# Gate and up of a gated feed-forward: weights as the stationary operand, 256 tokens moving

## The chip, the cores and the metric

One core of a Trainium2 chip runs the whole program. The metric is device time in microseconds (us), from runs of the compiled program; a profile of one execution stands beside them. In the profile PE is TensorE's matmul, PEld its weight load, DVE VectorE, ACT ScalarE, POOL GpSimd and SP SyncE, whose queue issues the loads.

## The reference, cut to what matters

The model is two blocks of two layers each on x of 256 tokens by 1024 features. A layer of the first block is a feed-forward, an attention mixer and another feed-forward; a layer of the second is a mixer and a feed-forward with modulated norms. So there are six feed-forwards, each with 2816 hidden columns:

```python
def swiglu(h, w_gate, w_up, w_down):
    return (jax.nn.silu(h @ w_gate) * (h @ w_up)) @ w_down
...
        x = x + 0.5 * swiglu(h, ffn1_w_gate[l], ffn1_w_up[l], ffn1_w_down[l])
```

All of it is float32.

## The kernel before

**Products.** A float32 product is made of three float32r products: each operand is split into a high part and the rest (`xh`, `xl` for the tokens, `whi`, `wlo` for weights, `hth`, `htl` for the hidden values), and `mm3` issues high by high, high by low, low by high. Each product is one matmul instruction with its own weight load. The operand named `lhsT` is stationary (128x128), `rhs` moves.

**Tokens.** The 256 tokens are two tiles of 128. `xh` and `xl` hold the normed input transposed, 128 features by 8 k-tiles by 256 tokens. `proj` (line 609) takes 128 tokens as the stationary operand and 512 weight columns as the moving one.

**A feed-forward** (`ffn`, line 619) goes over 11 chunks of 256 hidden columns. A chunk's gate and up columns, 256 each, lie side by side in the 512 moving columns, and its weights come in two units (k-tiles 0 to 3 and 4 to 7) of 128x2048. For each token tile 24 matmuls fill one PSUM bank (tag `mm`, two of them); `post` (line 624) takes silu of the gate half on ScalarE and multiplies by the up half on VectorE into `hch`, with tokens on the partitions. `turn` (line 636) then transposes the chunk with four 128x128 transposes on TensorE into a PSUM tile (tag `tp`) and splits it from there into `hth` and `htl`, hidden columns on the partitions, which is the form that `down` (line 649) needs as its stationary operand. `down` issues 24 matmuls of 512 moving columns for a chunk, four chunks late (`LAG`), into four PSUM banks (tag `y`). Chunks 0 and 1 have an order of their own at the start, chunks 2 to 10 run in one loop (line 683); the last four `down`s come after it. The very first feed-forward has its norm's factors `r` applied after the products.

**Weights** are a stream of 1 MB units in order of use (`WStream`, up to 4 units split and 3 raw ones): SP loads a unit, ScalarE copies it into `whi`, VectorE subtracts into `wlo`, each in two halves.

**Order of the work.** `Plan` records every instruction and then issues them in the order of a list schedule with an assumed cost for each (`cost`): every engine takes, of what is ready, the most urgent. `priorities` (line 306) computes the urgencies, and keeps work beside the main products from falling more than `LATE` behind them; it knows main products by a moving width of 512 (line 317). Between products `slot` issues steps of other work that the second block needs early (tables, modulation rows).

Since a helper issues everything, all profile rows carry line L304; the tile names tell the groups apart.

Of the kernel before, what the change touches and what calls it, by code (L numbers as in the profile page):

```python
# [18 lines left out]
P = 128  # L19
# [12 lines left out]
# order of the output projections' (token tile, group of 256 columns); pools of attention's PSUM beside them  # L32
# [3 lines left out]
# engines of the copies out of PSUM, in turn  # L36
COPY = "a"
# the first two units come in CUTS pieces, FIRST of them before the second token tile; up to NCUT in two;
# splits of the others in SPLITS pieces
CUTS, FIRST, NCUT, SPLITS = 4, 2, 5, 2  # L40
# products that warm the array's clock while the first loads are under way
WARM = 8
# the list schedule
# [4 lines left out]
class Pool:  # L48
    """A tile pool whose tiles the plan knows: which slots they share and how many there are."""
# [23 lines left out]
class Plan:  # L73
    """Records the program in its order, then issues it in the order of a list schedule:
    every engine takes, of the instructions whose operands are there, the one needed soonest."""
# [72 lines left out]
    def cost(self, eng, method, args, kw, aps):  # L148
        """ns on the engine, ns on the DMA rings, activation table."""
        if method == "dma_start":  # L150
            return (1000 if eng == "gpsimd" else 475), 4 * int(np.prod(list(args[0].shape))) / 360, None
        n = max(int(np.prod(list(a.shape)[1:])) for k, a in aps)
        psum = any(a.space == PSUM for _, a in aps)
        if eng == "tensor":
            if method == "transpose":
                return 109, 0, None
            n = kw["rhs"].shape[-1]
            if kw["rhs"] is self.cold:
                return 4 * max(107, n / 1.2 + 2), 0, None
            if kw["rhs"].dtype == F32R:  # L160
                return n / 2.4 + 2.5, 0, None
            return 2 * max(107, n / 1.2 + 2), 0, None
        if eng == "scalar":
            extra = 93 * sum(1 for k, _ in aps if k in ("bias", "scale", "accum_out"))
            f = args[2] if len(args) > 2 else kw.get("func")
            return 0.833 * n + (52 if psum else 94) + extra, 0, "silu" if f == AF.Silu else "exp" if f in (AF.Exp, AF.Ln) else None
        if eng == "vector":
            fast = method in ("tensor_copy", "tensor_scalar", "memset") and not psum
            scalars = sum(1 for k, _ in aps if k not in (0, 1, "out", "in_")) if method == "tensor_scalar" else 0
            scalars += sum(1 for k, _ in aps if k == 2) if method == "scalar_tensor_tensor" else 0  # L170
            return n * (0.52 if fast else 1.042) + 68 + 62 * scalars, 0, None
        if eng == "gpsimd":
            if kw.get("op") == ALU.pow:
                return 300 + 165 * n, 0, None
            return 148 + (3.15 if method == "tensor_copy" else 2.11) * n, 0, None
        return 60, 0, None

# [1 line left out]
    def order(self, prio):  # L179
        """List schedule: every engine starts, of what can start within DELTA of the soonest, the most urgent.  # L180
        A tile may take a slot before its turn if the program's order could still go on from there."""
# [41 lines left out]
        def slot_time(i):  # L223
            """When the slots of the tiles that op i touches first are free; None: not now."""
# [81 lines left out]
    def priorities(self):  # L306
        """How long before the end an op has to start, by a schedule from the end; no later than LATE behind
        the large products it was recorded with, and the first loads in their order."""
# [3 lines left out]
        for _ in range(ITERS):  # L312
# [3 lines left out]
            for i, o in enumerate(ops):  # L316
                if o[1] == "matmul" and o[3]["rhs"].shape[-1] == 512:
                    main = p[i]
                p[i] = max(p[i], main - LATE)
# [4 lines left out]
    def backward(self, start):  # L324
        """List schedule from the end; a tile waits for the one that had its slot in the program's order."""
# [52 lines left out]
class WStream:  # L378
    """Weights in the order of their use: load ahead, split into hi + lo float32r parts ahead."""
# [9 lines left out]
    def cuts(self, i, n):  # L389
        """The first units come in pieces: the products start the sooner."""  # L390
# [12 lines left out]
    def _load(self, pieces=None):  # L403
        """The next unit, or only the next pieces of it."""
# [47 lines left out]
class Net:  # L452
# [80 lines left out]
    def rstd2(self, ss):  # L533
        """(ss[0] + ss[1] + eps) ** -0.5: the two halves' parts of a mean of squares."""
# [6 lines left out]
    def norm(self, t, gain, shift=None):  # L541
        """rms_norm(x_t) * gain (+ shift)"""
# [18 lines left out]
    def first_xT(self, t, gain):  # L561
        """xh/xl columns of token tile t := transpose of x_t * gain; the tokens' factors come after the products."""
# [28 lines left out]
    def m(self, n, name, dt=F32):  # L591
        """One of the shared 2 KB slots."""
# [16 lines left out]
    def proj(self, ps, n, t, half, u, kts=4):  # L609
        """ps[128, n] += x^T k-tiles of one weight unit [128, kts, n]."""  # L610
# [8 lines left out]
    def ffn(self, ydone, mid, pre, r=None):  # L619
# [26 lines left out]
        def mmps():  # L646
            return self.ps.tile([P, 512], F32, tag="mm", name="mm")

# [34 lines left out]
        for c in range(2, NCH):  # L683
            u = [W.next() for _ in range(2)]
            for t in range(2):
                ps = mmps()
                for half in range(2):
                    self.proj(ps, 512, t, half, u[half])
                    if t == 1:
                        W.done(u[half])  # L690
                    self.slot()
                post(c, t, ps)
                if t == 0:
                    if c == 2:
                        turn(0)
                    turn(c - 1)
# [10 lines left out]
        for t in range(2):  # L707
            for i, d in enumerate(range(NCH - LAG, NCH)):
                down(d, t, us[i])
                if t == 0 and i == 0:  # L710
# [25 lines left out]
    def slot(self):  # L736
        """Between the products of a feed-forward: one step of the work that block 2 needs early."""
# [12 lines left out]
    def copy(self, out, in_):  # L750
        """PSUM -> SBUF, on the engines in turn."""
# [27 lines left out]
    def skew(self, name, src, offset, nh, rows, n):  # L779
        """Every head's n values once per row, each row SKEW after the one before: read at SKEW - 1 they slide."""  # L780
# [5 lines left out]
    def diff_lambda(self, l):  # L786
        """-lambda on every partition; the output gain times (1 - lambda_init)."""
# [17 lines left out]
    def na_bias(self, l):  # L805
        """8 * (relative bias, or -1e30 outside the window), [token of a tile, tile, head, key]."""
# [19 lines left out]
    def prep(self, t, ps, segs, w, rope, dstT, flag):  # L826
        """Heads' norms, gains and rotations of a [128, n] projection, then its transpose."""
# [54 lines left out]
    def job(self, kind, l, h, q, k, vh, col, bias=None):  # L882
        """softmax(q k / 8 + bias) v for one head, both token tiles of queries."""
# [32 lines left out]
    def turn_p(self, p):  # L916
        """[query, (tile, key)] -> [key of a tile, (query tile, key tile, query)]"""
# [54 lines left out]
    def turn_o(self, g, flag):  # L972
        """o columns of one group of 256, transposed and split for the output projection."""
# [135 lines left out]
    def modulation(self):  # L1109
        """Rows of block 2's norms: gain * (1 + scale), shift, gate * post gain, twice per layer."""  # L1110
# [52 lines left out]
    def t5_bias(self):  # L1163
        """8 * (table[bucket(q - k)], or -1e30 above the diagonal), keys of the tile before | own tile."""
# [34 lines left out]
    def gated_residual(self, t, y, i):  # L1199
        """x_t += gate * rms_norm(y) * gain"""  # L1200
# [11 lines left out]
    def rot2(self, X, nh, t):  # L1212
        """Rotary positions on [128, nh, 32]."""
# [7 lines left out]
    def latents(self, l, t, ps, st):  # L1221
        """Norms of the latents and their transposes, rotated shared key, forget logits."""
# [27 lines left out]
    def forget(self, l, st):  # L1250
        """F, the cumulative log forget gates: min(z, 0) - log(1 + e), e = exp(-|z|), log(1 + e) = 2 artanh(e / (2 + e)); the fox biases 8 * (F[q] - F[k]), or -1e30 above the diagonal."""
# [26 lines left out]
    def qk_fox(self, t, ps, dst, st):  # L1278
        """Queries [q, 8 F, 1] and keys [k, 1, -8 F], transposed: their products are 8 (q k / 8 + F[q] - F[k])."""
# [32 lines left out]
    def latent_heads(self, t, ps, part, st):  # L1312
        """Four heads of the up-projections: queries (part 0) or keys and values (part 1), transposed."""
# [22 lines left out]
    def causal_job(self, kind, q, k, vh, col, bias, scale):  # L1336
        """Causal softmax(q k * scale + bias) v for one head; bias comes divided by the scale."""
# [30 lines left out]
    def group_norm(self, l, g0, ng):  # L1368
        """rms_norm over groups g0 .. of 256 columns of o, then transposed, times the gain, and split."""
# [188 lines left out]
def pack(inputs):  # L1558
    """Weights laid out as the units are read: every partition's part of a unit is contiguous."""
# [7 lines left out]
    def gu(g, u):  # L1567
        g = g.reshape(2, 4, P, NCH, 256).transpose(3, 0, 2, 1, 4)
        u = u.reshape(2, 4, P, NCH, 256).transpose(3, 0, 2, 1, 4)
        return np.concatenate([g, u], axis=-1).reshape(2 * NCH, P, UW)  # L1570

    stack = lambda f: np.stack([f(l) for l in range(L)])
    for i in (1, 2):
        o[f"gu{i}"] = stack(lambda l: gu(a[f"ffn{i}_w_gate"][l], a[f"ffn{i}_w_up"][l]))
# [37 lines left out]
def shape_consts():  # L1612
    """Positions, masks and multiplicities: functions of the shapes alone."""
# [51 lines left out]
```

## Time and profile before

| | |
|---|---|
| median of 3 runs | 1675.52 us (1671.84 to 1676.18) |
| profiled execution, its span | 1670.4 us; the page gives no other time for it |
| PE busy | 1646.5 us (99%), 7912 matmuls |
| PEld busy | 1346.0 us (81%), 7912 loads |
| DVE busy | 1086.1 us (65%) |
| ACT busy | 841.8 us (50%) |
| DMA | 335.78 MB, mean 201 GB/s |

The span runs from the first to the last instruction of the profiled execution. Matmuls overlap in the records (a matmul's recorded duration is longer than the distance to the next one's start), so what a matmul costs is read from the distance between starts, not from its duration.

### The profile page before, as it was taken

Reading aid. Unit: us, or ns where it says so; the run is one execution under the profiler, and the core shown is the slowest. Engines: PE = TensorE matmul, PEld = TensorE weight load, DVE = VectorE, ACT = ScalarE, POOL = GpSimd, SP = SyncE. Lnnn points to the kernel's source line nnn. Section 1 sums busy time; section 2 is a strip of 40 time slices with the busy share of each in tenths; the row PEclk is TensorE's granted clock in tenths of the full one; section 3 lists DMA queues with packets and bytes.
Section 4 is the critical chain, followed back from the end, with each engine's and each line's share of the span. In section 5 each row is a group of like instructions: output and inputs, shape, how many; then the busy total and the mean of one; then the engine's idle time right before and its main releaser. Section 6 shows DMA issues by size and latency. Waiting matters only on the chain.

```text
span 1670.4 us, 21333 instructions
## 1 busy us (share of the span) xinstructions
PE 1646.5 (99%) x7912; PEld 1346.0 (81%) x7912; DVE 1086.1 (65%) x1956; ACT 841.8 (50%) x1384; POOL 166.3 (10%) x205
## 2 busy tenths in 40 slices
PE   9989999999999999999999999999999999999998
PEld 7868877888888888887788888888888888888886
DVE  6557788577677776777857655656754476585553
ACT  6544456554444444446554444576643358664442
POOL 0000056000000000026500000120000012000000
PEclk9999999999999999998999999999999999999999
DMA  8587762257776877763328645541655445255451
GB/s 302 210 272 274 262 224 102 76 212 298 271 270 250 306 266 268 288 221 121 127 86 316 229 171 192 173 174 51 239 181 199 150 167 202 96 181 190 171 201 51
DMA packets 81884, 335.78 MB, mean 201 GB/s; under 512 B 17136, under 2 KB 19700, under 8 KB 50676
## 3 DMA queue, kind: packets, MB, share of 16 engines
q1 hardware_dynamic: 81780, 334.42, 55.7%
q8 instruction: 62, 1.02, 0.2%
q14 instruction: 42, 0.34, 0.1%
HBM read 333.29 MB, written 2.84 MB: 201 GB/s over the span
## 4 chain that ended last, share of the span: by engine, by line
PE 94%; DVE 2%; POOL 2%; DMA 1%; ACT 1%; issue 0%; SPq 0%; POOLq 0%; DVEq 0%; ACTq 0%
PE mm L304 55%; PE y L304 27%; PE att L304 6%; PE tp L304 6%; DMA raw<-in_gu 1%; POOL rs L304 1%; DVE wlo L304 1%; POOL qk L304 0%; POOL rot L304 0%; DVE o L304 0%; DVE qk L304 0%; DVE ms L304 0%; DMA t5t<-in_t_table 0%; ACT xh L304 0%; DVE qkT L304 0%
## 5 line engine op out<-in xcount | busy, mean ns | idle before, releaser
L304 DVE TENSOR_TENSOR wlo<-raw,whi 128x1024 fp32r<-128x1024 f32 (+2 forms) x516 | 607.5, 1211 | 273.9 <-ACT whi L304 272.4
L304 ACT CAST whi<-raw 128x1024 fp32r<-128x1024 f32 (+2 forms) x516 | 512.5, 1035 | 319.3 <-PE mm L304 132.3
L304 PE MATMUL mm<-whi,xh 128*128 128x512 f32 (+2 forms) x1376 | 552.5, 402 | 2.8 <-ACT whi L304 1.8
L304 PE MATMUL mm<-wlo,xh 128*128 128x512 f32 (+2 forms) x1376 | 543.2, 395 | 0.2 <-DVE wlo L304 0.2
L304 PE MATMUL mm<-whi,xl 128*128 128x512 f32 (+2 forms) x1376 | 539.6, 393 | 0.8 <-DVE xl L304 0.8
L304 PEld LDWEIGHTS mm<-whi,xl 128*128 128x128 f32 x1376 | 259.5, 189 | 61.4 <-DVE xl L304 1.8
L304 PEld LDWEIGHTS mm<-whi,xh 128*128 128x128 f32 x1376 | 259.5, 189 | 61.4 <-ACT whi L304 2.1
L304 PEld LDWEIGHTS mm<-wlo,xh 128*128 128x128 f32 x1376 | 259.7, 189 | 55.3 <-DVE wlo L304 0.9
L304 PE MATMUL y<-whi,htl 128*128 128x512 f32 x528 | 207.5, 393 | 0.0
L304 PE MATMUL y<-wlo,hth 128*128 128x512 f32 x528 | 207.2, 392 | 0.0
L304 PE MATMUL y<-whi,hth 128*128 128x512 f32 x528 | 207.2, 394 | 0.0
L304 ACT ACTIVATE sil<-mm 128x256 f32<-128x256 f32 x110 | 42.3, 384 | 224.1 <-PE mm L304 223.3
L304 POOL TENSOR_TENSOR rs<-rs,mhalf 128x1 f32<-128x1 f32 x28 | 26.1, 932 | 1286.2 <-DVE rs L304 1286.2
L304 DVE CUSTOM_DVE_ANT_0 ada<-ada,act 128x512 f32<-128x512 f32 x192 | 128.7, 691 | 13.5 <-DMA ada<-in_ada 13.2
L304 PEld LDWEIGHTS y<-wlo,hth 128*128 128x128 f32 x528 | 99.7, 189 | 22.7 <-issue 1.3
L304 PEld LDWEIGHTS y<-whi,hth 128*128 128x128 f32 x528 | 99.5, 189 | 21.5 <-ACT whi L304 0.2
L304 PEld LDWEIGHTS y<-whi,htl 128*128 128x128 f32 x528 | 99.7, 189 | 21.3
L304 DVE TENSOR_TENSOR hch<-mm,sil 128x256 f32<-128x256 f32 x110 | 46.4, 421 | 89.7 <-ACT sil L304 89.4
L304 PE MATMUL att<-qkT 64*128 64x256 f32 (+6 forms) x368 | 65.7, 320 | 1.5 <-DVE qkT L304 1.2
L304 POOL TENSOR_TENSOR rs<-ms,mhalf 128x2 f32<-128x2 f32 (+3 forms) x34 | 50.9, 1500 | 136.2 <-DVE ms L304 134.6
L304 PEld LDWEIGHTS att<-V,pt 128*128 128x128 f32 x448 | 58.6, 193 | 6.4 <-ACT pt L304 2.3
L304 PE MATMUL att<-V,pt 128*128 128x65 f32 (+1 forms) x448 | 59.1, 270 | 1.8 <-ACT pt L304 1.8
(158 smaller groups left out, 1390.5 us busy)
## 6 DMA issues: line engine op xcount, KB each, us to landing
raw<-in_gu SPq DMA_DIRECT2D x127, 1024.0 KB, 4.9
raw<-in_dn SPq DMA_DIRECT2D x66, 1024.0 KB, 4.9
ada<-in_ada SPq DMA_DIRECT2D x192, 256.0 KB, 5.3
raw<-in_in SPq DMA_DIRECT2D x32, 1024.0 KB, 4.9
raw<-in_out SPq DMA_DIRECT2D x16, 1024.0 KB, 4.8
row<-moddram SPq DMA_DIRECT2D x12, 512.0 KB, 6.6
raw<-in_in2a SPq DMA_DIRECT2D x4, 840.0 KB, 4.3
raw<-in_gu SPq DMA_DIRECT2D x6, 512.0 KB, 5.8
```

The lines of the kernel that those rows point to most:

```text
L304: getattr(getattr(self.nc, eng), method)(*args, **kw)
```

## The change

Chunks 2 to 10 of every feed-forward but the first (45 of 66 chunks) compute gate and up with the weights as stationary operand and all 256 tokens moving. A unit now holds 128 hidden columns: for each of 8 k-tiles 128 gate columns and 128 up columns (the host lays the weights out so; the units' size and number stay). `columns(c, f)` issues, for one unit, 24 matmuls for the gate and 24 for the up half of one PSUM bank; silu and product give `hch` with hidden columns on the partitions already, so that it is split from SBUF, with no transpose. The `turn`s of those chunks go; chunks 0 and 1 keep theirs, now both after the first unit of chunk 2. `priorities` also takes a matmul with a weight as stationary operand for a main product. Comments were dropped throughout; they are left out here.

```diff
@@ priorities
-                if o[1] == "matmul" and o[3]["rhs"].shape[-1] == 512:
+                if o[1] == "matmul" and (o[3]["rhs"].shape[-1] == 512 or o[3]["lhsT"].tensor.name.startswith(("whi", "wlo"))):
                     main = p[i]
@@ ffn
+        def columns(c, f):
+            u = W.next()
+            _, wh, wl = u
+            ps = mmps()
+            mm = nc.tensor.matmul
+            for part in range(2):
+                out = ps[:, part * S:part * S + S]
+                for k in range(8):
+                    cs = slice(k * 256 + part * P, k * 256 + part * P + P)
+                    mm(out, lhsT=wh[:, cs], rhs=self.xh[:, k], start=k == 0, stop=False)
+                    mm(out, lhsT=wl[:, cs], rhs=self.xh[:, k], start=False, stop=False)
+                    mm(out, lhsT=wh[:, cs], rhs=self.xl[:, k], start=False, stop=k == 7)
+                if part == 1:
+                    W.done(u)
+                self.slot()
+            if f == 0:
+                hs[c] = self.m(512, "hch")
+            s = self.m(256, "sil")
+            h = hs[c][:, f * S:f * S + S]
+            nc.scalar.activation(s, ps[:, 0:S], AF.Silu)
+            nc.vector.tensor_tensor(h, ps[:, S:2 * S], s, op=ALU.mult)
+            if f == 1:
+                hi, lo = (self.m(512, n, F32R) for n in ("hth", "htl"))
+                self.split(hi, lo, hs.pop(c))
+                hT[c] = tuple(a.rearrange("p (f q) -> p f q", f=2) for a in (hi, lo))
...
         for c in range(2, NCH):
-            u = [W.next() for _ in range(2)]
-            for t in range(2):
-                ps = mmps()
-                for half in range(2):
-                    self.proj(ps, 512, t, half, u[half])
-                    if t == 1:
-                        W.done(u[half])
-                    self.slot()
-                post(c, t, ps)
-                if t == 0:
-                    if c == 2:
+            if r is None:
+                for f in range(2):
+                    columns(c, f)
+                    if c == 2 and f == 0:
                         turn(0)
-                    turn(c - 1)
+                        turn(1)
+            else:
...
-                if t == 0 and i == 0:
+                if t == 0 and i == 0 and r is not None:
                     turn(NCH - 1)
@@ pack
-    def gu(g, u):
-        g = g.reshape(2, 4, P, NCH, 256).transpose(3, 0, 2, 1, 4)
-        u = u.reshape(2, 4, P, NCH, 256).transpose(3, 0, 2, 1, 4)
-        return np.concatenate([g, u], axis=-1).reshape(2 * NCH, P, UW)
+    def gu(g, u, turned=True):
+        parts = [w.reshape(2, 4, P, NCH, 256).transpose(3, 0, 2, 1, 4) for w in (g, u)]
+        o = np.concatenate(parts, axis=-1).reshape(2 * NCH, P, UW)
+        if turned:
+            parts = [w.reshape(8, P, 2 * NCH, P).transpose(2, 1, 0, 3) for w in (g, u)]
+            o[4:] = np.concatenate(parts, axis=-1).reshape(2 * NCH, P, UW)[4:]
+        return o
```

## Rows read from the trace of the kernel before

**Rows 1.** The page: busy us (share of the span) xinstructions of each engine.

```profile
PE 1646.5 (99%) x7912; PEld 1346.0 (81%) x7912; DVE 1086.1 (65%) x1956; ACT 841.8 (50%) x1384; POOL 166.3 (10%) x205
```

**Rows 2.** The page: the chain that ended last, by engine and by line.

```profile
PE 94%; DVE 2%; POOL 2%; DMA 1%; ACT 1%; issue 0%; SPq 0%; POOLq 0%; DVEq 0%; ACTq 0%
PE mm L304 55%; PE y L304 27%; PE att L304 6%; PE tp L304 6%; DMA raw<-in_gu 1%; POOL rs L304 1%; DVE wlo L304 1%; POOL qk L304 0%; POOL rot L304 0%; DVE o L304 0%; DVE qk L304 0%; DVE ms L304 0%; DMA t5t<-in_t_table 0%; ACT xh L304 0%; DVE qkT L304 0%
```

**Rows 3.** Waits of PE: us in total, times, longest.

```profile
PE tp L304 <- DMA t5t<-in_t_table: 5.8, 1, 5.8
...
PE mm L304 <- ACT whi L304: 1.8, 1, 1.8
...
PE mm L304 <- DVE wlo L304: 0.2, 1, 0.2
```

**Rows 4.** PE's groups by shape: count, busy us, mean ns, idle before.

```profile
L304 PE MATMUL mm<-whi,xh 128*128 128x512 f32 x1312 | 531.2, 405 | 2.6 <-ACT whi L304 1.8 <-ACT xh L304 0.7
...
L304 PE MATMUL tp<-ident,hch 128*128 128x128 f32 x264 | 39.1, 273 | 0.0
...
L304 PE MATMUL mm<-whi,xh 128*128 128x256 f32 x32 | 9.6, 301 | 0.0
```

**Rows 5.** PE's timeline, one chunk of the second feed-forward: start us, us, instruction.

```profile
430.15 0.39 PE L304 MATMUL mm<-whi,xh 128*128 128x512 f32 x1
...
435.76 0.60 PE L304 MATMUL tp<-ident,hch 128*128 128x128 f32 x4
436.12 0.47 PE L304 MATMUL mm<-whi,xh 128*128 128x512 f32 x1
436.43 0.39 PE L304 MATMUL mm<-wlo,xh 128*128 128x512 f32 x1
...
441.79 0.40 PE L304 MATMUL y<-whi,hth 128*128 128x512 f32 x1
...
447.29 0.39 PE L304 MATMUL mm<-whi,xh 128*128 128x512 f32 x1
```

**Rows 6.** PE's timeline, two matmuls of a down product, nine apart.

```profile
427.20 0.39 PE L304 MATMUL y<-whi,htl 128*128 128x512 f32 x1
...
429.24 0.39 PE L304 MATMUL y<-whi,htl 128*128 128x512 f32 x1
```

**Rows 7.** Timeline of PE and PEld in the first mixer's projection of 256 columns.

```profile
303.72 0.28 PE L304 MATMUL mm<-wlo,xh 128*128 128x256 f32 x1
303.73 0.19 PEld L304 LDWEIGHTS mm<-whi,xl 128*128 128x128 f32 x1
303.85 0.28 PE L304 MATMUL mm<-whi,xl 128*128 128x256 f32 x1
303.85 0.19 PEld L304 LDWEIGHTS mm<-whi,xh 128*128 128x128 f32 x1
...
306.24 0.28 PE L304 MATMUL mm<-wlo,xh 128*128 128x256 f32 x1
```

**Rows 8.** PE's timeline in that mixer's attention: eight matmuls of 65 columns.

```profile
307.91 1.10 PE L304 MATMUL att<-V,pt 128*128 128x65 f32 x8
308.86 0.28 PE L304 MATMUL tp<-ident,p 128*128 128x128 f32 x1
```

**Rows 9.** DVE's and ACT's groups by shape in 430.15 to 447.29, one chunk.

```profile
L304 DVE TENSOR_TENSOR wlo<-raw,whi 128x1024 fp32r<-128x1024 f32 x6 | 7.1, 1221 | 3.8 <-ACT whi L304 3.8
...
L304 ACT CAST whi<-raw 128x1024 fp32r<-128x1024 f32 x6 | 6.0, 1046 | 5.5 <-issue 3.3 <-PE mm L304 2.2
...
L304 DVE TENSOR_TENSOR htl<-tp,hth 128x512 fp32r<-128x512 f32 x1 | 0.7, 685 | 0.0
...
L304 ACT CAST hth<-tp 128x512 fp32r<-128x512 f32 x1 | 0.6, 587 | 0.1
```

**Rows 10.** Busy us (instructions) by stretch: two chunks; then clock, DMA share, GB/s.

```profile
430.15:447.29 17.14, 17.14 (x78) 13.91 (x76) 12.10 (x21) 7.24 (x9) 0.00 (x0) 1.00 0.73 276
447.29:464.42 17.13, 17.13 (x77) 13.91 (x76) 12.02 (x21) 7.24 (x9) 0.00 (x0) 1.00 0.74 277
```

More of the change, by code (lines that the diff above doesn't have):

```diff
@@ L683, in ffn @@
         for c in range(2, NCH):
-            u = [W.next() for _ in range(2)]
-            for t in range(2):
-                ps = mmps()
-                for half in range(2):
-                    self.proj(ps, 512, t, half, u[half])
-                    if t == 1:
-                        W.done(u[half])
-                    self.slot()
-                post(c, t, ps)
-                if t == 0:
-                    if c == 2:
-                        turn(0)
-                    turn(c - 1)
+            if r is None:
+                for f in range(2):
+                    columns(c, f)
+                    if c == 2 and f == 0:
+                        turn(0)
+                        turn(1)
+            else:
+                u = [W.next() for _ in range(2)]
+                for t in range(2):
+                    ps = mmps()
+                    for half in range(2):
+                        self.proj(ps, 512, t, half, u[half])
+                        if t == 1:
+                            W.done(u[half])
+                        self.slot()
+                    post(c, t, ps)
+                    if t == 0:
+                        if c == 2:
+                            turn(0)
+                        turn(c - 1)
             if c == 2:
@@ L1565, in kpack @@
         return w.reshape(w.shape[0] // (kt * P), kt, P, n).transpose(0, 2, 1, 3).reshape(-1, P, kt * n)
-    def gu(g, u):
-        g = g.reshape(2, 4, P, NCH, 256).transpose(3, 0, 2, 1, 4)
-        u = u.reshape(2, 4, P, NCH, 256).transpose(3, 0, 2, 1, 4)
-        return np.concatenate([g, u], axis=-1).reshape(2 * NCH, P, UW)
+    def gu(g, u, turned=True):
[5 more added lines that the diff above has]
+        return o
     stack = lambda f: np.stack([f(l) for l in range(L)])
     for i in (1, 2):
-        o[f"gu{i}"] = stack(lambda l: gu(a[f"ffn{i}_w_gate"][l], a[f"ffn{i}_w_up"][l]))
+        o[f"gu{i}"] = stack(lambda l: gu(a[f"ffn{i}_w_gate"][l], a[f"ffn{i}_w_up"][l], (i, l) != (1, 0)))
         o[f"dn{i}"] = stack(lambda l: kpack(a[f"ffn{i}_w_down"][l], 2))
```

## The prediction

> **What bounds the kernel now.** I read the page's busy shares first: PE 99% of the span, VectorE 65%, ScalarE 50% [rows 1]. A busy PE proves little where records overlap, so I went on to the chain of waits: 94% of it is PE, 55% in `mm` tiles and 27% in `y` tiles [rows 2]. The list of PE's waits closes the point: its longest is 5.8 us, once, for a small table in the first feed-forward, and those for weights are 1.8 and 0.2 us in the whole run [rows 3]. So the reader is to see an engine that always has its next instruction ready, and for which time is the sum of the distances between the starts of its instructions. Nothing that shortens another engine's work helps here, and every added nanosecond between PE's starts is paid.
>
> What a distance is stands in the timeline, not in the mean durations: `mm` records are 405 ns long [rows 4], but inside a chunk they start far closer. One chunk of the loop runs from 430.15 to 447.29 us: 24 matmuls for one token tile take 435.76 - 430.15 = 5.61 us, the four transposes 436.12 - 435.76 = 0.36 us, 24 more matmuls 441.79 - 436.12 = 5.67 us, and the down product 447.29 - 441.79 = 5.50 us [rows 5]. The matmul behind the transposes is 436.43 - 436.12 = 0.31 us from its successor where 0.23 is usual, so the transposes really cost 0.36 + 0.08 = 0.44 us, and the 48 gate and up matmuls 5.61 + 5.67 - 0.08 = 11.20 us, 233.3 ns each. The next chunk is as long to 0.01 us, at a granted clock of 1.00, which is the level of 2.4 GHz [rows 10].
>
> **The change part by part.** A changed chunk keeps its multiplications and its split instructions. It swaps 48 matmuls of 512 columns for 96 of 256, and drops four transposes. There are five feed-forwards of nine such chunks, so 45.
>
> Removed: 45 x 0.44 = 19.8 us of transposes. Of the 264 transposes of `hch` [rows 4] 84 stay (44 of the first feed-forward, 8 in each of the others). All of it lay on PE, which never waits, so all of it comes back.
>
> Swapped: the trace has the new shape. The mixers project 256 columns with a 128x128 stationary operand and the same three products [rows 4]. Between 303.72 and 306.24 us lie 21 starts, seven k-tiles of three: 2.52 / 21 = 120.0 ns each [rows 7]. Hence 96 x 120.0 = 11.52 us in place of 11.20: 0.32 us more in a chunk, 45 x 0.32 = 14.4 us. The columns stream for the same time (at 2.4 GHz, 256 take 106.7 ns and 512 take 213.3); the surplus per instruction is 13.3 ns at 256 and 20.0 ns at 512, and there are twice as many instructions.
>
> Net: 14.4 - 19.8 = -5.4 us. It is a small difference of two terms, and 1 ns in the new distance moves it by 45 x 96 ns = 4.3 us. So that distance is the whole question, and I bound it. In the mixers' rows the tokens are stationary and the weights move; in the change it is the other way round, which no row shows. A surplus isn't the same for every stationary tile: the down product, with `hth` stationary, has starts (429.24 - 427.20) / 9 = 226.7 ns apart, 13.3 ns over its columns [rows 6], against 20.0 ns with `xh`. From below: if the surplus halves with the columns, as half of a down matmul would have it, the distance is 113.3 ns, a chunk's gate and up 10.88 us, and the sum 45 x (10.88 - 11.64) = -34 us. Lower than that is not to be had: eight matmuls of only 65 columns take (308.86 - 307.91) / 8 = 119 ns each [rows 8], so a new stationary operand per instruction has a floor near there whatever moves. From above: the 20.0 ns that `xh` shows at 512, now at 256, gives 126.7 ns, 12.16 us and 45 x 0.52 = +23.6 us. I take 120.0, because its row has the same three tiles, the same shape and the same three-product order.
>
> The Trainium skill (TensorE: Matmul & The Clock Gate, "Back-to-back issue gap") gives a warm matmul N / 2.4 + 2.5 ns. By it the distances would be 109.2 and 215.8 ns, an estimate from that page, a chunk would gain 0.31 us and the kernel 14 us. The rows disagree at both widths (120.0 and 233.3 or 226.7), so the sum doesn't use it.
>
> Weight loads: each chunk issues 48 more. In the rows of 256 columns a load starts within 0.01 us of the matmul before its own and is over 0.19 us later, which is beyond that matmul's slot, and the matmuls still keep 120 ns [rows 7]; so the cost of loads is inside the 120.0, not beside it. The same page ("LDWEIGHTS (loading the stationary operand)") has a load take P / 1.2 ns, 106.7 for 128 columns, by which 256 columns of matmul hide it with nothing to spare. The trace has no case of it being late, but this is what the slower rival rests on.
>
> Other engines: silu, product and split stay in number. `hth` and `htl` (587 and 685 ns from PSUM) now read SBUF; half of a weight's split from SBUF (1046 / 2 and 1221 / 2) says 523 and 611 [rows 9], so not dearer, and they are needed four chunks later. VectorE has 12.1 us of work and ScalarE 7.2 in a chunk of 17.1 [rows 10], which the change doesn't move by 1 us; if that cover went, the first thing late would be a `wlo`, now the stationary operand, whose load would wait at the head of PE's queue with every later matmul behind it. It has more room than before: a chunk's two units are used one after the other, 5.76 us each, instead of both across 11.6 us, and a half unit takes 1.05 us to copy and 1.22 to subtract. SP issues the same units of 1 MB in the same number; at 0.73 of the DMA engines [rows 10] a chunk 0.12 us shorter changes nothing. PSUM's `mm` banks turn over every 5.76 us instead of 5.6.
>
> The two `turn`s of chunks 0 and 1 move by half a chunk, unchanged in cost; their readers come two chunks later. The planner sees other urgencies and may order the mixers' side work otherwise; PE's waits there are a few us in all [rows 3], so I give this 0, with 4 us either way.
>
> **Sum.** 1670.4 - 5.4 = 1665.0 us of span. The median of the runs lies 5.1 us above the span of the profiled execution; I keep that: 1670.1 us.
>
> **The rivals.**
>
> A, the surplus shrinks: with the weights stationary the distance is 113 to 118 ns. For it: the surplus depends on the stationary tile, 13.3 against 20.0 ns at one width [rows 5, 6]. Against: the floor of rows 8, and 120.0 with weights on the other side. At 116.7 ns, half of 233.3, the gate and up stay at 11.20 us and the transposes are pure gain: -19.8 us, 1655.7 us.
>
> B, the load becomes the pace and the kernel is slower: a load of weights has to come in while only 256 columns stream, and with `xh` and `xl` moving the surplus is the larger one. Place: each of the 4320 new matmuls. Price: 126.7 ns, +23.6 us, 1699.1 us. It decides from 121.3 ns on (11.64 us / 96), which is only 1.3 ns above my value. For it: 20.0 ns with `xh` at 512. Against: the same tile at 256 shows 13.3.
>
> C, loads no longer overlap at all. Rows 7 show 120 ns with a load of 190 ns in each, so a serial load would have to come from the swap alone; its price would be at least 4320 x 107 ns, 462 us. The Trainium skill (same page, "The mechanism") says that a load overlaps matmuls in flight only when the row groups differ; here all use the full array and the rows show the overlap, so I leave it 1%.
>
> D, the change does not do what it says, the transposes staying or the planner undoing it elsewhere: -5.4 becomes 0 or so. That is inside the 4 us of scatter and I fold it into the main case.
>
> **How the numbers follow.** Main case (118.5 to 121.5 ns) 0.50, A 0.26, B 0.23, C 0.01. The main case spans -11.9 to +1.1 us, and with the scatter -14 to +4. Measurement tells about 0.3% of 1675.5, 5 us. A is faster throughout, half of the main case is; the other half is within 5 us; B is slower except for its nearest part. So faster 0.51, same 0.27, slower 0.22. For 8 in 10 the range goes into A to 115.5 ns (-25 us) and into B to 125 ns (+16 us): 1650 to 1692; the main case's own range is 1661 to 1680.
>
> **What would show it.** Right: in a chunk of the new profile PE's starts are 120 ns apart in `mm` and 227 in `y`, no transposes of `hch` between, and a chunk takes 17.0 us for 17.14. The `hch` transposes number 84, matmuls 7912 + 2160 - 180 = 9892, PE still has no wait to speak of. Wrong: another distance (each nanosecond is 4.3 us), PE waiting for `wlo` in the feed-forwards, or mixers of another length than before.

## The result, and the profile after

The changed kernel takes 1656.67 us (median of four runs, 1654.93 to 1659.75), the kernel before, run beside it, 1673.96 us (1671.84 to 1676.18): a ratio of 0.9896 with a 95% interval of 0.9879 to 0.9914. The spans of the two profiled executions differ by 15.4 us, 1655.0 against 1670.4. The prediction had 1670.1 us in a range of 1650 to 1692, with faster as the likeliest sign. The sign and the main mechanism came as forecast; the gain is three times as large (15.4 us of span where 5.4 was forecast).

The page's busy shares and the first line of its chain of waits (shares of the span), to be read against [rows 1, 2]:

```profile
PE 1631.8 (99%) x9892; PEld 1433.2 (87%) x9892; DVE 1090.4 (66%) x1956; ACT 833.4 (50%) x1384; POOL 166.3 (10%) x205
...
PE 94%; DVE 2%; POOL 2%; DMA 1%; ACT 1%; issue 0%; SPq 0%; POOLq 0%; DVEq 0%; ACTq 0%
```

PE has the 9892 matmuls that were forecast and is still 94% of the chain; no other engine took its place. PE's waits (us in total, times, longest) say the same, to be read against [rows 3]:

```profile
PE tp L304 <- DMA t5t<-in_t_table: 5.5, 1, 5.5
...
PE mm L304 <- DVE wlo L304: 0.5, 2, 0.2
```

The weights, now the stationary operand, are waited for by 0.5 us in all. PE's groups by shape, where [rows 4] had 1312 of the second row's kind and 32 of 256 columns:

```profile
L304 PE MATMUL mm<-xh,whi 128*128 128x256 f32 x1440 | 404.6, 281 | 0.0
...
L304 PE MATMUL mm<-whi,xh 128*128 128x512 f32 x592 | 241.5, 408 | 1.9 <-ACT whi L304 1.2 <-ACT xh L304 0.7
```

The names before the shape are moving operand first, stationary second: 1440 matmuls of each product now have 256 columns of `xh` or `xl` moving, and 720 fewer have 512 columns of a weight. Of the transposes of `hch` 84 are left, as one row of that tile's instructions (count, then ns least/median/most, first and last start) shows:

```profile
L304 PE MATMUL tp<-ident,hch x84: 270/272/273, 37.8 to 1492.1; 128*128 128x128 f32 x84
```

What decides is the distance between starts. PE's timeline (start us, us, instruction) over one chunk of the second feed-forward, against [rows 5]:

```profile
411.52 0.28 PE L304 MATMUL mm<-xh,whi 128*128 128x256 f32 x1
...
422.92 0.39 PE L304 MATMUL y<-whi,hth 128*128 128x512 f32 x1
...
428.39 0.28 PE L304 MATMUL mm<-xh,whi 128*128 128x256 f32 x1
```

From 411.52 to 422.92 us lie 96 matmuls: 11.40 us, 118.7 ns each, where the prediction took 120.0. The down product runs from 422.92 to 428.39, 5.47 us where it was 5.50. A chunk is 16.87 us for 17.14. The windows of this chunk and the next one (us; busy us and instructions of PE, PEld, DVE, ACT, POOL; granted clock, DMA share, GB/s), against [rows 10]:

```profile
411.52:428.39 16.87, 16.87 (x121) 15.90 (x120) 12.28 (x22) 7.06 (x9) 0.00 (x0) 1.00 0.78 279
428.39:445.26 16.87, 16.87 (x122) 15.90 (x120) 12.35 (x22) 7.07 (x9) 0.00 (x0) 1.00 0.82 286
```

The work of DVE (12.1 before) and ACT (7.2 before) hardly moved, and the granted clock is 1.00 in these stretches of both kernels, so the clock has no part in what a chunk gains.

Where the 15.4 us of span lie can be read from landmarks on PE. The normalised input of each feed-forward is transposed (`tp` from `hn`), one token tile at a time, at its start. Before, the second tile's group of the second feed-forward and the first tile's of the third stand at

```profile
359.61 1.03 PE L304 MATMUL tp<-ident,hn 128*128 128x128 f32 x8
...
535.50 1.03 PE L304 MATMUL tp<-ident,hn 128*128 128x128 f32 x8
```

and after the change at

```profile
358.44 1.03 PE L304 MATMUL tp<-ident,hn 128*128 128x128 f32 x8
...
531.91 1.03 PE L304 MATMUL tp<-ident,hn 128*128 128x128 f32 x8
```

The feed-forward between them went from 175.89 to 173.47 us, 2.42 us less, which is nine chunks of 0.27. Five of them make 12.1 us. Ahead of them the changed kernel is 1.2 us early (358.44 against 359.61), and one mixer, between two later groups of this kind, takes 141.32 instead of 142.85 us. That makes 14.8 of the 15.4.

### The profile page after: what moved, and what is told of

Read it like the earlier page. It is cut to its first block, busy times and chain, and to the rows that moved or that the text cites. A ratio compares the mean times of both kernels' runs of the same rounds, so it can differ in the third digit from the quotient of the medians.

```text
span 1655.0 us, 25146 instructions
## 1 busy us (share of the span) xinstructions
PE 1631.8 (99%) x9892; PEld 1433.2 (87%) x9892; DVE 1090.4 (66%) x1956; ACT 833.4 (50%) x1384; POOL 166.3 (10%) x205
## 4 chain that ended last, share of the span: by engine, by line
PE 94%; DVE 2%; POOL 2%; DMA 1%; ACT 1%; issue 0%; SPq 0%; POOLq 0%; DVEq 0%; ACTq 0%
PE mm L304 56%; PE y L304 27%; PE att L304 6%; PE tp L304 5%; DMA raw<-in_gu 1%; POOL rs L304 1%; DVE wlo L304 1%; POOL rot L304 0%; POOL qk L304 0%; DVE o L304 0%; DVE qk L304 0%; DVE ms L304 0%; ACT xh L304 0%; DVE xl L304 0%; DMA t5t<-in_t_table 0%
## 5 line engine op out<-in xcount | busy, mean ns | idle before, releaser
L304 PE MATMUL mm<-xh,whi 128*128 128x256 f32 x1440 | 404.6, 281 | 0.0
L304 PE MATMUL mm<-xh,wlo 128*128 128x256 f32 x1440 | 404.4, 281 | 0.0
L304 PE MATMUL mm<-xl,whi 128*128 128x256 f32 x1440 | 404.3, 281 | 0.0
L304 PEld LDWEIGHTS mm<-xh,whi 128*128 128x128 f32 x1440 | 271.6, 189 | 1.4
L304 PEld LDWEIGHTS mm<-xh,wlo 128*128 128x128 f32 x1440 | 271.3, 188 | 1.4
L304 PEld LDWEIGHTS mm<-xl,whi 128*128 128x128 f32 x1440 | 271.8, 189 | 0.0
L304 PE MATMUL mm<-whi,xh 128*128 128x512 f32 (+2 forms) x656 | 262.7, 401 | 2.1 <-ACT whi L304 1.2
L304 PE MATMUL mm<-wlo,xh 128*128 128x512 f32 (+2 forms) x656 | 257.7, 394 | 0.6 <-DVE wlo L304 0.5
L304 PE MATMUL mm<-whi,xl 128*128 128x512 f32 (+2 forms) x656 | 255.5, 392 | 0.8 <-DVE xl L304 0.8
L304 PEld LDWEIGHTS mm<-wlo,xh 128*128 128x128 f32 x656 | 123.9, 189 | 26.1 <-DVE wlo L304 1.6
```

The source lines that it names most:

```text
L304: getattr(getattr(self.nc, eng), method)(*args, **kw)
```

## Experiments

The main theory was that the change gains the transposes and loses what 96 distances of 256 columns (from one start to the next) cost over 48 of 512. What was open was why these distances are 118.7 and 233.3 ns, and not something else. Distances below are those of `mm` in the feed-forwards' chunks.

**1. The transposes alone.** The kernel before, with the transposes of `hch` left out in the 45 chunks; `h` itself is split, so the down product has untransposed data. In `turn(c)`:

```diff
+            h = hs.pop(c)
+            if r is None and c >= 2:
+                hi, lo = (self.m(512, n, F32R) for n in ("hth", "htl"))
+                self.split(hi, lo, h)
+                hT[c] = tuple(a.rearrange("p (f q) -> p f q", f=2) for a in (hi, lo))
+                return
             tp = self.tp().rearrange("p (f q) -> p f q", f=2)
-            h = hs.pop(c)
```

> The kernel before without the four transposes of chunks 2 to 10 in the five later feed-forwards; the hidden values are split as they stand, so the down product multiplies the wrong way round (its output is not the reference's). Gate and up stay 512 wide. My theory: the transposes lie wholly on PE, 45 x 0.44 us = 19.8 us, ratio 0.988. Rival: what the timeline shows between the first transpose and the next matmul is all there is, 45 x 0.36 = 16 us, and the matmul after them keeps its longer distance.

Measured: 1651.27 us, ratio 0.9866 [0.9842, 0.9889], span 1650.3, which is 20.1 us under the span before. Its timeline in one chunk:

```profile
429.91 0.39 PE L304 MATMUL mm<-whi,xh 128*128 128x512 f32 x1
...
441.11 0.40 PE L304 MATMUL y<-whi,hth 128*128 128x512 f32 x1
...
446.59 0.39 PE L304 MATMUL mm<-whi,xh 128*128 128x512 f32 x1
```

Gate and up without transposes take 441.11 - 429.91 = 11.20 us, the figure that the prediction worked out as 5.61 + 5.67 - 0.08, so the 0.44 us of transposes in a chunk is right. The 20.1 us of span agree with the term of 19.8; by the medians it is 24.0 us (1651.27 against 1675.31 beside it), and spans of one kernel scatter by some 5 us, so the agreement to 0.3 us is chance and the chunk is the evidence.

**2. The other shape alone.** The kernel before, still with the tokens stationary and with the transposes, but gate and up each as 256 columns, so that twice as many instructions issue:

```diff
-                for half in range(2):
-                    self.proj(ps, 512, t, half, u[half])
+                for j in range(2):
+                    for half in range(2):
+                        if r is None:
+                            self.proj256(ps, j, t, half, u[half])
...
```

(`proj256` is the loop of `proj` over columns `j * 256` to `j * 256 + 256`; the planner counts these matmuls as it counted those of 512.)

> The kernel before with the tokens still stationary, but each 512-wide gate and up matmul of those 45 chunks made as two of 256 (gate columns first, then up columns), transposes kept. If the distance belongs to the tokens as stationary operand, 120.0 ns as in the mixers' rows: 45 x 0.32 = 14.4 us slower than before. If the distance is one of the width alone, 118.7 ns as in the changed kernel: 45 x 0.19 = 8.7 us slower. Either way this is the cost half of the change by itself.

Measured: 1677.88 us, ratio 1.0021 [1.0005, 1.0037], span 1674.5. Its timeline:

```profile
423.74 0.28 PE L304 MATMUL mm<-whi,xh 128*128 128x256 f32 x1
...
429.50 0.60 PE L304 MATMUL tp<-ident,hch 128*128 128x128 f32 x4
...
435.68 0.40 PE L304 MATMUL y<-whi,hth 128*128 128x512 f32 x1
...
441.15 0.28 PE L304 MATMUL mm<-whi,xh 128*128 128x256 f32 x1
```

Forty-eight matmuls take 429.50 - 423.74 = 5.76 us, 120.0 ns each; the chunk is 17.41 us for 17.14, which over 45 chunks is 12.2 us. The span grew by 4.1 only. The rest was given back at another place: the planner issued the load of the small table `t5t` earlier, at 84.6 us in place of 92.4, and the wait of 5.8 us for it [rows 3] is gone, with the slow stretch behind it (experiment 7). In this kernel, and then before, the load itself:

```profile
L304 SPq DMA_DIRECT2D t5t<-in_t_table x1: 417/417/417, 84.6 to 84.6; - x1
```

```profile
L304 SPq DMA_DIRECT2D t5t<-in_t_table x1: 314/314/314, 92.4 to 92.4; - x1
```

So the 120.0 of the mixers' rows holds for tokens stationary in the feed-forwards too, and the change's 118.7 came in with the exchange of operands; what in the exchange does it is taken up in experiment 6. And a total that moves by 4 us can hide a term of 12: the landmarks have to be read, not the total.

**3. Is the load of the stationary operand the pace (rival B)?** The changed kernel, with 128 tokens moving, twice as many matmuls and loads for the same columns:

```diff
-                for k in range(8):
+                for t in range(2):
+                    q = slice(t * P, t * P + P)
+                    for k in range(8):
...
-                    mm(out, lhsT=wh[:, cs], rhs=self.xh[:, k], start=k == 0, stop=False)
+                        mm(out[:, q], lhsT=wh[:, cs], rhs=self.xh[:, k, q], start=k == 0, stop=False)
```

> The changed kernel with each 256-wide matmul made as two of 128 tokens, so that a load goes with every 128 columns. It asks for the pace of the weight loads. If the load is the pace of the 256-wide matmuls already (my rival B), 128 wide comes out near 115 to 120 ns too, and the kernel is 45 x 96 x 118 ns = 510 us slower. If columns are the pace at 256, 128 wide is 53 + 13 = 67 ns and the kernel is 45 x 96 x 15 ns = 65 us slower.

Measured in one run: 2107.17 us. Its timeline:

```profile
440.26 0.22 PE L304 MATMUL mm<-xh,whi 128*128 128x128 f32 x1
...
461.65 0.45 PE L304 MATMUL y<-whi,hth 128*128 128x512 f32 x1
```

A chunk's 192 matmuls take 21.39 us, 111.4 ns each. Half the columns cost 94% of the time, so at 128 columns the pace is set by what each instruction costs, whatever its columns: its load, by my reading, though every matmul here has one and nothing separates the two. At 256 that pace is near, but not it, since 118.7 is above 111.4 (113.7, which occurs below, is too). Rival B did not come about, with 7 ns to spare. The time agrees: 45 x 96 x (2 x 111.4 - 118.7) ns is 450 us, and the kernel took 450.5 us more. The prediction's own floor, "near 119" from matmuls of 65 columns [rows 8], falls with this run.

**4. Alignment (a theory that fell).** By the order of allocation, `xh` lies at byte 46944 of each partition and the weights at 161472. The place of `xh` less that of the weights is 160 modulo 512 (this is what "difference" means below), while `hth` and `htl`, which show 226.7 in `y`, differ from the weights by 0. The first theory was that `xh` off a boundary of 64 bytes is what costs 6.6 ns per matmul of 512. Both kernels, with 32 bytes more in a small tile ahead of `xh` and 32 more in `V`, which lies behind `xl`, so that every large tile lies on 64 bytes; `xh` moves by 32 bytes, the weights and all else behind `V` by 64 (the difference becomes 128):

```diff
-        gain = self.const.tile([P, 8], F32, name="gain0")
+        gain = self.const.tile([P, 16], F32, name="gain0")[:, 0:8]
...
-        self.V = self.keep.tile([P, 2, 16, 65], F32, name="V")
+        self.V = self.keep.tile([P, 2088], F32, name="V")[:, 0:2080].rearrange("p (t h d) -> p t h d", t=2, h=16)
```

The kernel before:

> The kernel before with two pads of 32 bytes in SBUF, so that xh, xl, the weights and the hidden tiles all begin at multiples of 64 bytes (before, xh and xl lie 32 bytes past one, the others on one). Theory: the 20.0 ns over the columns at 512 come from where xh and xl lie; then gate, up and projections fall from 233.3 to 226.7 ns as in the down product, 3936 matmuls x 6.7 ns = 26 us faster. Rival: they come from adding 24 matmuls in a row into one PSUM bank, where the down product changes banks every three; then nothing changes.

The changed kernel:

> The changed kernel with the same two pads. Theory of the place: its remaining 512-wide matmuls with xh fall by 6.7 ns (about 1780 of them, 12 us), and the 4320 of 256 columns, where xh and xl now move, fall below 118.7 ns if the place of the moving tile counts too (each ns 4.3 us), or stay if only the stationary tile's place counts. Rival, the PSUM bank: no change from the changed kernel, ratio to before 0.990.

Measured: 1671.96 us, ratio 0.9984 [0.9969, 0.9998], for the kernel before, and 1663.89 us, 0.9947 [0.9926, 0.9967], for the changed one, some 7 us slower than without this edit. The timeline of the first:

```profile
409.49 0.39 PE L304 MATMUL mm<-whi,xh 128*128 128x512 f32 x1
...
413.67 0.40 PE L304 MATMUL mm<-whi,xh 128*128 128x512 f32 x1
```

Eighteen starts in 4.18 us are 232.2 ns; over longer stretches it is 232.7. Alignment isn't it: both were aligned, the one stayed and the other rose, to 119.6 ns on the average (118.6 to 119.9 by stretch). In the changed kernel that is 0.76 us in each of the five feed-forwards; the rest of the 7 us is one mixer, 131.62 us between the landmarks where it took 127.17. But that the distance moved at all, with nothing changed except the places of tiles, left the difference of the two places as the candidate. (The expectation's rival, 24 matmuls in a row into one PSUM bank, falls with experiment 5, which leaves that order as it is.)

**5. Difference 0 modulo 512.** The same edit with `V` of 2120 elements. The kernel before:

> The kernel before with 32 bytes of padding ahead of xh and 160 behind it, so that xh and xl start at the same byte offset modulo 512 as the weights, as hth and htl do by themselves (before, xh and xl lay 160 bytes past the weights' offset, in the run with both on multiples of 64 it was 128). Theory of the relative offset: the 512-wide matmuls with xh come 226.7 ns apart as in the down product instead of 233.3, 3936 x 6.7 ns = 26 us faster than before. Rival, the offset only rearranges single distances: 232 to 234 ns again and within 4 us of before.

The changed kernel:

> The changed kernel with the same padding. Theory of the relative offset: the 256-wide distance with weights stationary leaves 118.7 ns downward (down to 113.3 to 116.7, that is 9 to 23 us less than the changed kernel) and the remaining 512-wide ones fall to 226.7 (12 us). Rival: 118 to 121 ns and the time of the changed kernel within 8 us.

Measured: 1651.76 us, ratio 0.9865 [0.9843, 0.9887], span 1652.3, for the kernel before, and 1657.34 us, 0.9907 [0.9884, 0.9930], span 1653.1, for the changed one. The kernel before, with this edit:

```profile
409.50 0.39 PE L304 MATMUL mm<-whi,xh 128*128 128x512 f32 x1
...
414.26 0.39 PE L304 MATMUL mm<-whi,xh 128*128 128x512 f32 x1
...
414.94 0.60 PE L304 MATMUL tp<-ident,hch 128*128 128x128 f32 x4
...
420.85 0.39 PE L304 MATMUL y<-whi,hth 128*128 128x512 f32 x1
...
426.29 0.39 PE L304 MATMUL mm<-whi,xh 128*128 128x512 f32 x1
```

Twenty-one starts in 4.76 us: 226.7 ns, exactly that of `y` [rows 6], with the transposes still there. Gate, up and transposes take 420.85 - 409.50 = 11.35 us, the chunk 16.79. Moving tiles by some bytes is worth 22 us to the kernel before (18 by the spans), more than the whole change; 26 had been expected. The weights' own place moved too in experiments 4 to 6, and the hidden tiles moved with them: there single distances of `y` keep a median of 227 ns in every run. So it is not the weights' place by itself that counts, but their place against that of `xh` and `xl`. The changed kernel gains nothing from it:

```profile
409.73 0.28 PE L304 MATMUL mm<-xh,whi 128*128 128x256 f32 x1
...
419.09 0.28 PE L304 MATMUL mm<-xh,whi 128*128 128x256 f32 x1
```

Seventy-eight starts in 9.36 us: 120.0 ns. Its chunk's windows row:

```profile
407.94:424.92 16.98, 16.98 (x122) 16.02 (x120) 12.33 (x22) 7.06 (x9) 0.00 (x0) 1.00 0.78 279
```

So at difference 0 the change makes a chunk longer, 16.98 for 16.79 us, and by the medians costs 5.6 us, though the two intervals still touch and the spans differ by 0.8 only; the longer chunk is the firmer evidence.

The Trainium skill (TensorE: Matmul & The Clock Gate, "Step-by-step: what each phase is for") says that TensorE has two independent read ports, so that loading the next stationary tile takes no read bandwidth from the running matmul. By that the operands' places should not matter to the pace, and here they do: 233.3 and 226.7 ns were measured for the same instructions, and only the places were different. That it is the load which the running matmul meets is not shown.

**6. Other differences, the changed kernel.** 64 and 448 with `V` of 2104 and 2136 elements; 256 with `V` allocated ahead of `xh`, and 8 elements more in `xl`:

> The changed kernel with xh and xl 64 bytes past the weights' offset modulo 512 (160 in the changed kernel, 128 and 0 in the two padded runs). I look at two distances: 512 wide with tokens stationary (233.3 at 160, 232.7 at 128, 226.7 at 0) and 256 wide with weights stationary (118.7 at 160, 120.0 at 128 and 0). Theory: the offset sets both and 64 lies with 128, near 232 and 120. Rival: only exact agreement at 0 is special, and everything else gives 233.3 and 118.7.

> The same with 256 bytes of offset. If what counts is the offset modulo 256 or less, it is like 0: 226.7 and 120.0. If modulo 512 or more, something else: 230 to 240 and 113 to 122.

> The same with 448 bytes of offset, which is 64 on the other side of 0. If the offset acts alike on both sides, the distances of the run with 64. If it matters which tile is ahead, others; a 256-wide distance under 116 ns here would be the way to gain with this change, since loads alone go at 111.4 ns (the run of 128 columns).

Measured, one run each: 1658.87, 1655.8 and 1645.54 us. The distances in ns that the runs gave: `mm` with 512 weights' columns moving (in the chunks not changed, or in the kernel before), with 256 weights' columns moving (the mixers' projections, stretches of 22 distances), and with 256 tokens moving:

| difference | 512, tokens stationary | 256, tokens stationary | 256, weights stationary |
|---|---|---|---|
| 160 (both kernels as they were) | 233.3 | 119.8 to 120.1 | 118.7 |
| 128 | 232.7 | 118.4 to 120.0 | 119.6 |
| 64 | 233.3 | 113.6 to 114.0 | 117.8 |
| 0 | 226.7 | 119.3 to 119.8 | 120.0 |
| 256 | 226.7 | 119.6 to 119.8 | 120.0 |
| 448 | 229.0 | 117.7 to 117.8 | 117.8, in parts 113 to 114 |

0 and 256 are alike. The two shapes don't want the same place: what is best for 512 is worst for 256. The best at 256 with tokens stationary is at 64, here 21 distances in 2.39 us, 113.8 ns each:

```profile
298.78 0.28 PE L304 MATMUL mm<-wlo,xh 128*128 128x256 f32 x1
...
301.17 0.28 PE L304 MATMUL mm<-wlo,xh 128*128 128x256 f32 x1
```

The two columns of 256 also answer what the exchange of operands did. Counted as stationary less moving operand, the difference is the table's with the tokens stationary and its opposite with the weights stationary, so an exchange turns 160 into 352, and 64 into 448. Where both orders were measured at the same such difference they agree near 120 at 0 and at 256 and near 117.8 at 448; at 64 the tokens as stationary operand give 114, the weights (the table's row of 448) 113 to 114 in parts and 117.8 elsewhere. So no run shows that the exchange by itself changes the pace; that 120.0 became 118.7 fits the turned difference, though 352 was not measured with the tokens stationary. At 448, an ordinary chunk and then the first unit of that feed-forward:

```profile
409.80 0.28 PE L304 MATMUL mm<-xh,whi 128*128 128x256 f32 x1
...
421.11 0.39 PE L304 MATMUL y<-whi,hth 128*128 128x512 f32 x1
```

```profile
369.72 0.28 PE L304 MATMUL mm<-xh,whi 128*128 128x256 f32 x1
...
375.18 0.60 PE L304 MATMUL tp<-ident,hch 128*128 128x128 f32 x4
```

Ninety-six in 11.31 us are 117.8 ns; 48 in 5.46 us are 113.7, near the low end of the prediction's bounds.

**7. Both kernels at their best place, without the wait for `t5t`.** The wait is one stall in the first feed-forward of 5.4 to 6.7 us in every run up to here but that of experiment 2. It costs more than its length. The kernel before, around it:

```profile
88.76 0.39 PE L304 MATMUL y<-whi,hth 128*128 128x512 f32 x1
94.96 1.43 PE L304 MATMUL tp<-t5oh,t5t 32*4 32x384 f32 x2 [5.81 <-DMA t5t<-in_t_table]
96.32 0.80 PE L304 MATMUL y<-wlo,hth 128*128 128x512 f32 x1
...
100.76 0.39 PE L304 MATMUL y<-whi,htl 128*128 128x512 f32 x1
100.99 0.39 PE L304 MATMUL mm<-whi,xh 128*128 128x512 f32 x1
```

and in windows (columns as above) ahead of the wait, behind it, and later:

```profile
80.00:88.70 8.70, 8.70 (x41) 7.08 (x40) 4.58 (x8) 7.42 (x10) 0.00 (x0) 1.00 0.84 243
94.96:100.30 5.34, 5.34 (x11) 3.22 (x12) 0.00 (x0) 0.47 (x1) 0.00 (x0) 0.50 0.74 277
101.00:106.00 5.00, 5.00 (x23) 4.04 (x22) 2.36 (x2) 2.00 (x2) 0.00 (x0) 1.00 0.81 212
```

PE stood idle for 5.81 us, and the work behind it ran at a granted clock of 0.50, the level of 1.2 GHz: the eleven `y` matmuls from 96.32 to 100.99 take 4.67 us, where 11 x 227 ns would be 2.5. The edit records the table's product three slots later, on the changed kernel at 448 and on the kernel before at 0:

```diff
-        yield
+        for _ in range(4):
+            yield
```

> The changed kernel with the offset of 448 bytes, and the product for the small table t5 recorded three slots later, so that TensorE reaches it after its table has landed (in every run but one it waited 5.5 to 6.7 us there, and ran on at half clock for ten matmuls). Theory: the wait and the cold matmuls go, 8 us, on top of the 1645.5 us of the run with 448: about 1638 us, ratio to before 0.978. Rival: the planner puts the table's work where something else waits, and the time stays at 1645.

> The kernel before with offset 0 and the same later table: both of what the place and the wait cost it taken away, the transposes kept. Theory: 1651.8 - 8 = 1644 us, ratio 0.982. Beside the run above it says what the change is worth when each form lies at the best place found for it: by the chunks 11.32 us against 96 x 117.3 ns = 11.26, so 3 us for 45 chunks, and the rest of a difference would be something else. Rival: the change by itself is worth its first 17 us here too, and this run stays above 1655.

Measured: 1635.97 us, ratio 0.9770 [0.9748, 0.9792], span 1632.8, for the changed kernel, and 1642.84 us, 0.9808 [0.9785, 0.9832], span 1641.8, for the kernel before; the edit alone brings 11.0 and 10.5 us of span (from 1643.8 and 1652.3), of which 8.8 and 10.1 lie ahead of the first mixer; by the times it is 9.6 (from one run) and 8.9. The longest of PE's waits in the changed one:

```profile
PE tp L304 <- POOL qk L304: 3.5, 2, 1.8
```

No wait for `t5t` is left. With each at the best place found, the change is worth 6.9 us by the medians, though the two intervals still overlap. By the distances I expected 3. The traces show where the rest lies: the second and fourth feed-forwards are 0.55 us shorter each, which is the 3 us, but the third, fifth and last 1.5 to 1.7, and the mixers differ too. The first mixer takes 126.15 us in the kernel before and 121.44 in the changed one, between the landmarks

```profile
207.96 0.60 PE L304 MATMUL tp<-ident,hn 128*128 128x128 f32 x4
...
334.11 1.03 PE L304 MATMUL tp<-ident,hn 128*128 128x128 f32 x8
```

```profile
208.00 0.60 PE L304 MATMUL tp<-ident,hn 128*128 128x128 f32 x4
...
329.44 1.03 PE L304 MATMUL tp<-ident,hn 128*128 128x128 f32 x8
```

while the second is 1.7 us longer in the changed one. The change does not touch the mixers; part of the 6.9 us is the planner's order there.

## Why the prediction was right, and which term was off

**PE is the bound, and time is the sum of its distances.** Right. The shares, the chain and the waits are as before, and five feed-forwards of nine chunks at 0.27 us account for 12.1 of 15.4 us.

**19.8 us of transposes.** Right: experiment 1 gave 11.20 us for a chunk's gate and up without them, as worked out, and 20.1 us of span.

**+14.4 us for the swap, at 120.0 ns.** This is the mis-sized term. The distance is 118.7 ns, and 1.3 ns x 4320 is 5.6 us: the swap costs 45 x (11.40 - 11.20) = 9.0 us in place of 14.4. The row that the prediction rested on was sound for what it showed; experiment 2 repeats 120.0 with the tokens stationary in the feed-forwards. That the exchange of the operands might change it was said, and bounded by half of `y` below and the surplus of `xh` above, and 118.7 lies between, in the main case of 118.5 to 121.5. What the prediction did not see is that the row's distance belongs to the places of its operands, which the exchange turns round (experiment 6).

**Which tile causes the surplus.** The prediction saw that `mm` has 20.0 ns over its columns and `y` 13.3, and put it to the stationary tile. Experiment 5 shows that it is the tile's place against the other operand's, not the tile: at difference 0, which `y` has always had, `mm` has 13.3 as well.

**The floor near 119.** Wrong: 111.4 at 128 columns, 113.7 at 256. It did no harm, since the range reached to 115.5 ns and below.

**Loads, splits, PSUM, the other engines at nothing.** Right: 0.5 us of waits for `wlo`, and a chunk's DVE and ACT work within 0.3 us of before. `hth` and `htl` from SBUF, where the prediction expected 523 and 611 ns, are as dear as from PSUM [rows 9]; it is hidden. In the chunk from 411.52 to 428.39:

```profile
L304 DVE TENSOR_TENSOR htl<-hch,hth 128x512 fp32r<-128x512 f32 x1 | 0.7, 684 | 0.0
...
L304 ACT CAST hth<-hch 128x512 fp32r<-128x512 f32 x1 | 0.6, 622 | 0.0
```

**The planner's order, 0 with 4 us either way.** It came to 1.2 + 1.5 us of gain, inside that.

**The median over the span.** I carried over 5.1 us from the runs shown; beside the changed kernel it is 1.7 us (1656.67 - 1655.0). An execution's time is 1.7 to 1.9 us over its own span in nearly every run on record (2.1 to 2.2 in experiment 2), so the other 3.3 of the 5.1 were scatter: the profiled execution of the kernel before was a short one. From 1670.1 to 1656.67, 13.4 us, 5.6 are the distance, 1.3 the down product's 0.03 us a chunk, 2.7 the start and a mixer, 3.4 this difference of median and span, and 0.4 is not assigned.

**The rivals.** A, at its edge (113 to 118 ns), is what the changed kernel shows at a difference of 64 or 448; B needs 121.3, which no place tried gave; C and D did not happen. What none of them said is that the sign depends on where a buffer lies: the same change is worth 17 us at 160 and by the medians costs 5.6 at 0, because the kernel before has its worse distance at 160. The prediction weighed no places, and in this respect the right sign was luck.

## What to carry to other kernels

Where TensorE never waits, measure the distance between starts, over stretches of some twenty matmuls, for every pair of operands before restructuring: here it varied by 3% at 512 columns and 5% at 256 with the places of tiles, and moving them gave the kernel before 22 us, more than the change gave. A distance from a row with other operands, or from another place in memory, is a rough estimate and no value, when thousands of instructions multiply it. And look for the one stall with a slow stretch behind it: recording a small product three slots later was worth 9 to 10 us ahead of the first mixer, where the list shows a wait of 6 to 7.

## What the runs showed of the hardware that was not expected

- In these runs a matmul's pace depends on the difference of its two operands' byte places. 512 columns took 226.7 to 233.3 ns and 256 columns 113.6 to 120.1 at the differences in the table, which looks the same at 0 and at 256. Each load starts within 0.01 us of a matmul before its own [rows 7], so a likely cause is that the two streams meet in the memory; no run shows that directly, and why 113 occurs only in parts at 448 stays open. Differences between the six, and smaller moduli, were not tried.
- With 128 columns moving, matmuls with a new stationary tile each come 111.4 ns apart, hardly less than with 256.
- A wait of 5.8 us was followed by some 5 us at a granted clock of 0.50, in which eleven matmuls took 4.67 us in place of 2.5.
